# Expert weights of a mixture-of-experts layer: 2 MB loads in 16 KB rows, and a ring split into wide and narrow slots

## The chip, the cores and the metric

The kernel runs on one core of one Trainium2 chip. The metric is the device time of one execution in microseconds (us); lower is better. All data are float32 in the chip's main memory at the start, and the output goes back there. In this document 1 MB of a load is 1,048,576 bytes; the profile's own MB and GB/s are decimal, so that 1 MB at 424 GB/s takes 2.473 us.

## The reference, cut to what matters

Two transformer blocks over 256 tokens of width 1024. The first block and the mixer of the second take the first part of the kernel. What the change touches is the second block's expert layer: 64 experts in 8 groups, each token goes to two experts of one group, and every expert has three matrices of 2 MB each.

```python
def hier_moe(h, rg_w, rg_b, re_w, re_b, w_gate, w_up, w_down):      # 256 tokens, D = 1024
    g_prob = softmax(t @ rg_w + rg_b); p_group, g_sel = top_k(g_prob, 1)
    e_prob = softmax(logits of the chosen group's 8 experts); top_p, top_i = top_k(e_prob, 2)
    gate = p_group * top_p / sum(top_p); expert = g_sel * 8 + top_i
    ...
    def run_block(args):                                           # the tokens of one expert e
        xb = t_pad[tok]
        hb = silu(xb @ w_gate[e]) * (xb @ w_up[e])                 # w_gate, w_up: 64 x [1024, 512]
        return hb @ w_down[e]                                      # w_down: 64 x [512, 1024]
    # the outputs are added per token, weighted by gate; then a residual and a last norm
```

All 64 experts' matrices are read whatever the routing says: 64 x 6 MB = 384 MB.

## The kernel before, in words

The kernel has two kinds of stages. In the first (first block, and the second block's mixer, up to about 725 us) weights of 1 MB come through a **ring** of buffers in on-chip memory, named `raw`: a buffer is taken by `ring_tile`, filled by a load that SyncE (SP) issues, split into a high and a low part (`wh` by ScalarE, `wl` by VectorE), and multiplied three times by TensorE. A buffer is free for the next load when its last split is done. The order of the work on the compute engines is planned by `_Sched`; the order of the loads is simply the order in which the weights are used.

In the second stage, the experts, no weight is split: TensorE multiplies straight from the `raw` buffers. The loads are issued by `load_chunks` (line 1951) in the order of `seq`: for expert e four chunks, gate and up in turn, each [128 partitions x 4 x 512] (one half of a partition's eight rows of the matrix, 8 KB in one piece per partition), and then the two down chunks of expert e - 1, each [128 x 2 x 1024], made of two rows of 4 KB per partition. Every chunk is 1 MB and fits any buffer of the ring. The ring is one list: four buffers `ra`, six `rb` (since the first block's feed-forward), three `rc` (opened when the retention of the mixer, whose last tile is `oc`, is done), one `rd`, the two halves `xh` and `xl` of the transposed input, and, when the mixer's working memory is closed, five `re` and one `rf`: 22 buffers, 22 MB. SP issues loads strictly in order: a load whose buffer is not free holds back all behind it.

Per expert, TensorE does in this order: `gate_up(e)` (64 matmul passes of [128 x 32] by [128 x 256], the first half on the first two chunks, the second half on the other two), for every fourth expert the `gather` of the next four experts' tokens (32 matmuls on `oh`), `down(e - 1)` (32 passes on `gT`), and `turn(e)`, two transposes of the hidden tile `hh` into `gT`. `gate_up(0)` cannot start before the routing is through (the chain of small VectorE steps on tiles `r_...`, then `gather(0)`). For the last expert, `warm(1)` puts a matmul that nobody reads (`wk`) after every second k in `gate_up`, the down matrix comes in three pieces of columns (`LAST`), and `last_down` and the final norm follow.

Of the kernel before, what the change touches and what calls it, by code (L numbers as in the profile page):

```python
# [20 lines left out]
P = 128  # L21
# [5 lines left out]
# ---------------------------------------------------------------- layouts  # L27
# [9 lines left out]
PV["norm2p"] = _o        # feature 8 p + k in column k of partition p  # L37
# [10 lines left out]
def _const_tables():  # L48
    """Tables that depend on shapes alone, one row per partition."""
# [57 lines left out]
# columns of w_in  # L107
# [3 lines left out]
class _Engine:  # L111
    """An engine that also keeps its clock: an estimate of when its queue is through."""
# [34 lines left out]
class _Sched:  # L147
    """Emission order: a background of matrix products, with chains of small steps emitted
    between them as soon as their inputs are estimated to be there."""
# [24 lines left out]
    def lag(self, t):  # L174
        """the chain's result comes t later than its engine's time says."""
        self.end += t

    def step(self, g):
        """one step of g; True if it emitted anything or ended."""
        prev, e0, end0 = self.cur, self.emitted, self.end  # L180
        self.cur, self.end = g, 0.0
        try:
            next(g.g)
            alive = True
        except StopIteration:
# [14 lines left out]
    def force(self):  # L200
        """progress of the chain that is ready first."""
# [34 lines left out]
class _Cat:  # L236
    """k-tiles of several tiles as one."""
# [9 lines left out]
class _X:  # L247
    """a transposed operand as (high, low) parts; `ready` k-tiles of it are written."""
# [15 lines left out]
def kernel(ctx: ExitStack, tc: tile.TileContext, I: dict, out: bass.AP):  # L264
# [21 lines left out]
    # ------------------------------------------------------------ arithmetic helpers  # L286
# [14 lines left out]
    def mm3(o, l, r, start, stop):  # L301
        """o += l.T @ r with l = (high, low), r = (high, low)."""
# [21 lines left out]
    def split(hi, lo, src):  # L324
        """hi = the high part of src; lo = src - hi, a step later."""
# [4 lines left out]
    # ------------------------------------------------------------ constants, small inputs  # L330
# [28 lines left out]
    def warm(n):  # L359
        """products that nobody reads: they keep the tensor engine's clock up while it has to wait."""  # L360
# [4 lines left out]
    # ------------------------------------------------------------ weight stream  # L365
# [4 lines left out]
    def add_ring(pool, n, name, at=0):  # L370
        """n more slots, to be used after the next `at` ones."""
        ring[at:at] = [(pool, "%s%d" % (name, r)) for r in range(n)]

    def ring_tile(shape, name="raw"):
        slot = ring.pop(0)
        ring.append(slot)
        return slot[0].tile(shape, F32, name=name, tag=slot[1], bufs=1)
# [6 lines left out]
    def add_chunk(w, r0, nr, c0, ncol, mode):  # L384
        """rows r0.., columns c0.. of w, as [128, nr/128, ncol]; two pieces, cut by columns or by rows."""
# [38 lines left out]
    def get_piece(held=0):  # L424
        """the next piece, while `held` pieces before it are still to be used."""
# [7 lines left out]
    def convert(m):  # L433
        """the splits of the pieces that follow, piece m being the oldest in use."""
# [87 lines left out]
    # ------------------------------------------------------------ residual -> X^T (high, low), 1/rms  # L522
    def new_x():
        return _X([xpool.tile([P, 8, T], F32R, name="xh", tag="xh"), xpool.tile([P, 8, T], F32R, name="xl", tag="xl")], 0)
# [6 lines left out]
    def xt_steps(src, c, X, gname, ss):  # L531
        """columns c*256.. of src [128, 2, 1024] -> X^T k-tiles 2c, 2c+1, and sums of squares."""
# [24 lines left out]
    def rsqrt_ops(t, dst, src, scale):  # L557
        """dst = (src * scale + eps) ** -0.5: a guess from the bits, then Newton's steps."""
# [12 lines left out]
    def rsqrt_cols(t, dst, src, scale, cols):  # L571
        """the same for a few columns, each a [128, 1] with itself as a scalar: a shorter chain."""
# [55 lines left out]
    def tm_piece(pb, W, X, k0, K, first, last):  # L628
        """pb [128, 2, 256] += X^T.T @ W over k-tiles k0..k0+K."""
# [10 lines left out]
    def need(X, k):  # L640
        """k k-tiles of X; before the next piece is asked for, whose splits would get in their way."""
# [13 lines left out]
    def pair_tm(X, posts):  # L655
        """two chunks, the first halves first: the last k-tiles of X may come late."""
# [23 lines left out]
    # ================================================================ first block: mixer  # L680
# [26 lines left out]
    def norm_sums(srcs, pb):  # L707
        """token-major sums of squares over the 128 partitions: column 8 t + 2 h + i."""
# [17 lines left out]
    def norm_steps(items, inv, name):  # L726
        """items (x [128, 4, 256], gain or None, factor): x scaled in place by its heads' 1/norm."""
# [99 lines left out]
    def smalls():  # L827
        """forget, beta and decay logits, token-major."""
# [47 lines left out]
    # ---------------------------------------------------------------- gated delta rule  # L876
# [6 lines left out]
    def gdn():  # L883
# [5 lines left out]
        # cumulative decay inside chunks of 64  # L889
# [23 lines left out]
        et = smallA.tile([P, 32], F32, name="et")     # exp(gc) | exp(gl - gc) | exp(gl) rows  # L913
# [9 lines left out]
        # rows of beta * decay  # L923
# [4 lines left out]
        # k k^T and (k q^T), chunk by chunk  # L928
# [97 lines left out]
        free("s4", "s4", "g2")        # kbg, vb, U  # L1026
# [48 lines left out]
        free("g2", "g2", "s4", "s4", "s4", "s4")        # aT, S; qg, ktl, wT, u  # L1075

    def gdn_qg():
        """q scaled by exp(gc)."""
# [24 lines left out]
        # token-major k, v  # L1103
# [15 lines left out]
        free("s4", "s4", "s4")        # q, k, v  # L1119
# [6 lines left out]
    def gdn_out(i, po):  # L1126
# [24 lines left out]
        if sc.fin.get("yb", 0) == 1:  # L1151
            free("s4")        # gz
# [77 lines left out]
    def fox(i):  # L1230
# [22 lines left out]
    def fox_all():  # L1253
# [3 lines left out]
        free("s4", "s4", "s4")        # fq, fk, fv  # L1257

    # ---------------------------------------------------------------- stick-breaking, transposed scores
    def stick():  # L1260
# [3 lines left out]
        # banks: key tile 0, heads (0,1) and (2,3), all queries; key tile 1, all heads, queries 128..255  # L1264
# [11 lines left out]
        free("s4", "s4")        # sq, sk  # L1276
# [81 lines left out]
    # ---------------------------------------------------------------- gates x branch outputs, w_out  # L1358
# [32 lines left out]
    def bg_mix():  # L1391
        for n, (y, b, need) in enumerate((("yc", 2, 1), ("ya", 0, 2), ("yb", 1, 2))):
# [19 lines left out]
            free("s4", "s4", "s4", "s4")        # y, gates  # L1412
# [8 lines left out]
    # ================================================================ first block: attention over the memory  # L1421
# [70 lines left out]
    def mq_norm(c):  # L1492
        """1/rms of the queries of heads 2 c, 2 c + 1: column 2 h + i."""
# [55 lines left out]
    def bg_mo():  # L1549
        yield from banks(3, "mm")  # L1550
        pbs, W = [], []
        for c in range(3):        # the first two heads' part first
# [19 lines left out]
    # ================================================================ first block: conv ffn  # L1572
    pools = {}

    def to_ffn():
        a1.close()
        rawB = ctx.enter_context(tc.tile_pool(name="rawB", bufs=1))
        add_ring(rawB, NRB2, "rb", 2)
# [112 lines left out]
    # ================================================================ second block: retention and conv  # L1691
# [141 lines left out]
    def ret_out(n, po):  # L1833
# [17 lines left out]
        if sc.fin["rg"] == 2:  # L1851
            pools["a3r"].close()
            add_ring(ctx.enter_context(tc.tile_pool(name="rawC", bufs=1)), 3, "rc", 8)
# [48 lines left out]
    add_ring(ctx.enter_context(tc.tile_pool(name="rawD", bufs=1)), 1, "rd", 13)  # L1902
    ring[13 + 1:13 + 1] = [(xpool, "xh"), (xpool, "xl")]
# [24 lines left out]
    # expert weights: four chunks for gate and up, two for down, in the order of use  # L1928
    wg, wu, wd = I["w_gate_2"][0], I["w_up_2"][0], I["w_down_2"][0]
    LAST = (0, 512, 768, D)        # the last expert's down matrix comes in pieces of columns  # L1930
    chunks = {}
    nload = [0]
    seq = []
    for e in range(NE + 1):
        seq += [(e, r) for r in range(4) if e < NE] + [(e - 1, r) for r in (4, 5, 6)[:3 if e == NE else 2] if e > 0]

    def load_chunks(upto):
        """loads of expert chunks upto (exclusive); a slot is taken again once its last use is emitted."""
        while nload[0] < min(upto, len(seq)):
            e, r = seq[nload[0]]  # L1940
            if r < 4:
                src = (wg, wu)[r % 2][e].rearrange("(p k) n -> p k n", p=P)[:, (r // 2) * 4:(r // 2) * 4 + 4, :]
# [360 lines left out]
```

## Time and profile before

| what | value |
|---|---|
| median of 3 runs | 1670.82 us (1669.52 to 1933.18) |
| profiled execution, from first to last instruction (its span; no other time of it is given) | 1671.8 us |
| TensorE matmul busy | 1408.8 us, 84% |
| VectorE / ScalarE busy | 648.1 us, 39% / 446.5 us, 27% |
| moved by DMA | 516.74 MB, mean 309 GB/s |

The profile cuts the span into 40 slices of 41.8 us. For each it gives the busy share of an engine in tenths, the clock that TensorE was granted, the busy share of the 16 DMA engines and the GB/s that they moved. Slices 1 to 17 are the first stage, 19 to 40 the experts.

### The profile page before, as it was taken

How to read it: one execution, taken by the hardware profiler on the slowest of the kernel's cores; microseconds unless marked ns; L12 is line 12 of the kernel's file. 1: busy time of each engine (PE TensorE's matmuls, PEld its weight loads, DVE VectorE, ACT ScalarE, POOL GpSimd, SP SyncE). 2: the span in 40 equal slices, each digit the busy share in tenths (PEclk: the TensorE clock that was granted, in tenths of full speed). 3: DMA queues.
4: the chain of work that ended last, by engine and by line, in shares of the span. 5: the costliest groups of instructions: out<-in, count | busy, mean ns of one | idle time of the engine just before them, and what ended most of it. 6: DMA issues, size and time to landing. Idle time of an engine off the chain costs nothing. (4 is left out here: it accounts for less than half of the span.)

```text
span 1671.8 us, 30189 instructions
## 1 busy us (share of the span) xinstructions
PE 1408.8 (84%) x13017; PEld 1066.5 (64%) x13017; DVE 648.1 (39%) x1160; ACT 446.5 (27%) x821; POOL 78.8 (5%) x246
## 2 busy tenths in 40 slices
PE   8999999999999999898867767776786787777685
PEld 7999989989999989875534443443443444344242
DVE  5945356856777767742211111111111111111112
ACT  5643345546555554411100000000000000000001
POOL 1011110131100010200000000000000000000000
PEclk9999999999999999999988887988977987898888
DMA  8543225633855645669999999999999999999995
GB/s 286 175 129 102 77 88 184 208 126 130 301 198 180 216 155 177 237 274 414 423 424 424 424 424 424 424 424 423 423 425 424 424 424 424 424 423 424 424 424 227
DMA packets 170486, 516.74 MB, mean 309 GB/s; under 512 B 9248, under 2 KB 96688, under 8 KB 137584
## 3 DMA queue, kind: packets, MB, share of 16 engines
q1 hardware_dynamic: 169392, 511.90, 77.7%
q0 software_dynamic: 672, 2.66, 0.4%
q8 instruction: 104, 1.70, 0.4%
q10 hardware_dynamic: 288, 0.23, 0.1%
q14 instruction: 30, 0.25, 0.0%
HBM read 513.71 MB, written 1.05 MB: 308 GB/s over the span
## 5 line engine op out<-in xcount | busy, mean ns | idle before, releaser
L288 PE MATMUL pbmm<-raw,xt 128*32 128x256 f32 x4096 | 328.6, 448 | 90.0 <-DMA raw<-in_w_up_dram 73.0
L288 PEld LDWEIGHTS pbmm<-raw,xt 128*32 128x32 f32 x4096 | 156.4, 125 | 247.1 <-DMA raw<-in_w_up_dram 110.9
L122 DVE TENSOR_TENSOR wl<-raw,wh 128x1024 fp32r<-128x1024 f32 x202 | 248.6, 1233 | 129.5 <-PE pbmm L288 81.2
L288 PE MATMUL pbmm<-xh,wh 128*128 128x256 f32 x992 | 285.2, 288 | 0.0
L288 PE MATMUL pbmm<-xl,wh 128*128 128x256 f32 x992 | 279.4, 282 | 0.1
L288 PE MATMUL pbmm<-xh,wl 128*128 128x256 f32 x992 | 278.8, 281 | 0.0
L122 ACT ACTIVATE wh<-raw 128x1024 fp32r<-128x1024 f32 x202 | 213.5, 1060 | 235.1 <-PE pbmm L288 190.2
L122 DVE TENSOR_TENSOR hh<-hh,pbmm 64x256 f32<-64x256 f32 x64 | 27.2, 425 | 464.2 <-ACT hh L122 464.2
L288 PE MATMUL pbmm<-raw,gT 128*32 128x256 f32 (+2 forms) x2112 | 144.7, 401 | 55.7 <-DMA raw<-in_w_down_dram 54.6
L288 PEld LDWEIGHTS pbmm<-xh,wh 128*128 128x128 f32 x992 | 188.9, 190 | 2.1 <-issue 1.2
L288 PEld LDWEIGHTS pbmm<-xl,wh 128*128 128x128 f32 x992 | 188.5, 190 | 1.4 <-issue 0.7
L288 PEld LDWEIGHTS pbmm<-xh,wl 128*128 128x128 f32 x992 | 188.5, 190 | 0.0
L122 ACT ACTIVATE hh<-pbmm 64x256 f32<-64x256 f32 x64 | 24.0, 375 | 513.4 <-PE pbmm L288 513.4
L288 PE MATMUL pbmm<-oh,xres 128*128 128x128 f32 x512 | 131.4, 422 | 30.2 <-DVE oh L122 30.2
L288 PEld LDWEIGHTS pbmm<-oh,xres 128*128 128x128 f32 x512 | 124.5, 334 | 44.9 <-issue 43.5
L288 PEld LDWEIGHTS pbmm<-raw,gT 128*32 128x32 f32 x2112 | 64.9, 116 | 125.4 <-DMA raw<-in_w_down_dram 59.6
L122 DVE COPY ye<-pbmm 32x256 f32<-32x256 f32 (+2 forms) x138 | 56.2, 408 | 193.3 <-ACT ye L122 190.3
L122 ACT COPY ye<-pbmm 32x256 f32<-32x256 f32 x126 | 45.6, 362 | 289.6 <-PE pbmm L288 259.1
L288 PE MATMUL pbfg<-ye,Se 128*128 128x512 f32 (+1 forms) x132 | 65.9, 644 | 10.4 <-DVE ye L122 10.4
L122 DVE TENSOR_TENSOR xt<-pbmm,pv 128x512 f32<-128x512 f32 x32 | 22.1, 692 | 107.0 <-PE pbmm L288 107.0
L288 PEld LDWEIGHTS pbfg<-ye,Se 128*128 128x128 f32 x132 | 24.9, 208 | 39.9 <-DVE ye L122 20.7
L298 PE MATMUL pbmm<-cst,S 128*128 128x128 f32 x32 | 9.7, 400 | 43.2 <-DVE S L122 43.2
(442 smaller groups left out, 1690.6 us busy)
## 6 DMA issues: line engine op xcount, KB each, us to landing
raw<-in_w_up_dram SPq DMA_DIRECT2D x150, 1024.0 KB, 19.6
raw<-in_w_down_dram SPq DMA_DIRECT2D x138, 1024.0 KB, 19.7
raw<-in_w_gate_dram SPq DMA_DIRECT2D x128, 1024.0 KB, 19.7
raw<-in_w_in_dram SPq DMA_DIRECT2D x45, 1024.0 KB, 5.0
raw<-in_w_out_dram SPq DMA_DIRECT2D x4, 1024.0 KB, 5.0
raw<-in_w_mkv_dram SPq DMA_DIRECT2D x4, 1024.0 KB, 5.0
raw<-in_w_o_dram SPq DMA_DIRECT2D x4, 1024.0 KB, 5.2
raw<-in_w_oc_dram SPq DMA_DIRECT2D x2, 1024.0 KB, 5.3
```

The costliest lines, as they stand in the source:

```text
L122: r = f(*a, **k)
L288: PE.matmul(o, l, r, start=start, stop=stop, skip_group_check=True)
L298: PE.transpose(o, i, idt)
```

## The change: what it does

- Gate and up matrices of an expert come as one load each: 2 MB, [128 x 8 x 512], one row of 16 KB per partition. They go into **wide** buffers, which stand in a list of their own, `ring2`: one of `rc`, three of `rb` (the six of before in pairs), one of `xhl` (`xh` and `xl` are now one tile), and, appended later, two of `re`: 7 wide buffers, 14 MB.
- Down matrices still come as two loads of 1 MB, but with the rows of a partition next to each other: one row of 8 KB per partition. `turn` reads the hidden tile with a stride of two to match (not for the last expert, whose down pieces keep their old layout). They go into **narrow** buffers, which stay in `ring`: four `ra`, two `rd`, one `rg`, one `rf`: 8 MB.
- `load_chunks` takes the head of the list that the next load belongs to. If the chunk in that buffer has not been used by the program so far (its key is still in `chunks`), it returns.
- In the first stage the `rb` pairs are used as two halves of one tile.

All instructions of TensorE, VectorE, ScalarE and GpSimd stay in the same order; only SP's loads change.

```diff
+    class _Slot:
+        def __init__(self, pool, tag, wide=None, half=0):
+            self.pool, self.tag, self.wide, self.half, self.key = pool, tag, wide, half, None
+        def tile(self, shape, name):
+            if self.wide is None:
+                return self.pool.tile(shape, F32, name=name, tag=self.tag, bufs=1)
+            if self.half == 0:
+                self.wide["tile"] = self.pool.tile([P, 2, 2048], F32, name=name, tag=self.tag, bufs=1)
+            return self.wide["tile"][:, self.half].rearrange("p (a b) -> p a b", a=shape[1])
...
-        add_ring(rawB, NRB2, "rb", 2)
+        add_ring(rawB, NRB2 // 2, "rb", 2, wide=True)
...
-            add_ring(ctx.enter_context(tc.tile_pool(name="rawC", bufs=1)), 3, "rc", 8)
+            wide["c"] = slots(rawC, 1, "rc", True)
+            add_ring(rawC, 1, "rd", 8)
...
-        seq += [(e, r) for r in range(4) if e < NE] + [(e - 1, r) for r in (4, 5, 6)[:3 if e == NE else 2] if e > 0]
+        seq += [(e, r) for r in range(2) if e < NE] + [(e - 1, r) for r in (4, 5, 6)[:3 if e == NE else 2] if e > 0]
+    ring2 = wide["c"][:1] + [x for x in ring if x.wide is not None and x.half == 0] + [_Slot(xpool, "xhl", {})]
+    ring[:] = [x for x in ring if x.wide is None] + late
-    def load_chunks(upto):
-        while nload[0] < min(upto, len(seq)):
-            e, r = seq[nload[0]]
+    def load_chunks():
+        while seq:
+            e, r = seq[0]
+            rg = ring2 if r < 4 else ring
+            if rg[0].key in chunks:
+                return
+            slot = rg.pop(0)
+            rg.append(slot)
+            slot.key = seq.pop(0)
             if r < 4:
-                src = (wg, wu)[r % 2][e].rearrange("(p k) n -> p k n", p=P)[:, (r // 2) * 4:(r // 2) * 4 + 4, :]
-                t = ring_tile([P, 4, 512])
+                src = (wg, wu)[r][e].rearrange("(p k) n -> p k n", p=P)
+                t = slot.pool.tile([P, 8, 512], F32, name="raw", tag=slot.tag, bufs=1)
...
-                src = wd[e, (r - 4) * 256:(r - 3) * 256, :].rearrange("(k p) n -> p k n", p=P)
-                t = ring_tile([P, 2, D])
+                src = wd[e, (r - 4) * 256:(r - 3) * 256, :].rearrange("(p k) n -> p k n", p=P)
+                t = slot.tile([P, 2, D], "raw")
             SP.dma_start(t, src)
...
-    load_chunks(len(ring))
+    load_chunks()
     warm(31)
     wsp.close()
-    add_ring(rawE, 5, "re")
-    load_chunks(len(ring))
+    ring2 += slots(rawE, 2, "re", True)[::2]
+    load_chunks()
...
-    add_ring(ctx.enter_context(tc.tile_pool(name="rawF", bufs=1)), 1, "rf")
-    NR = len(ring)
-    load_chunks(NR)
+    ring += slots(rawE, 1, "rg") + slots(ctx.enter_context(tc.tile_pool(name="rawF", bufs=1)), 1, "rf")
+    load_chunks()
...
     def gate_up(e):
-        ck_ = [chunks.pop((e, r)) for r in range(4)]
+        w2 = [chunks.pop((e, r)) for r in range(2)]
...
-                w = ck_[(k // 4) * 2 + q // 2]
-                mm(gu[q * 32:(q + 1) * 32, 0:256], xt[:, k, es], w[:, k % 4, (q % 2) * 256:(q % 2) * 256 + 256],
+                mm(gu[q * 32:(q + 1) * 32, 0:256], xt[:, k, es], w2[q // 2][:, k, (q % 2) * 256:(q % 2) * 256 + 256],
                    k == 0, k == 7)
...
-            tr(pt[:, c * 64:(c + 1) * 64], h[64:, c * P:(c + 1) * P], ident[64:, 64:])
+            tr(pt[:, c * 64:(c + 1) * 64], hc[:, c], ident[64:, 64:])
...
     for e in range(NE):
-        load_chunks(4 * e + 2 * max(0, e - 1) + NR)
+        load_chunks()
```

SP's queue before, from the 13th of the expert loads: the end of the 22 loads that fill the ring, and the first two that use a buffer again. The number after `raw` is the buffer's use, and in brackets stand the counters that the load waits for (`DMAHW` the landing of an earlier load, `DVE`, `PE`, `Activation` and `Pool` the engine that used the memory last).

```order
L1951 DMA raw_8187<-in_w_gate_2_dram 128x2048 [waits DMAHW4_49,PE_49]
L1951 DMA raw_8189<-in_w_up_2_dram 128x2048 [waits DMAHW5_49]
L1951 DMA raw_8191<-in_w_down_2_dram 128x2x1024 [waits DMAHW6_49,DVE_49]
L1951 DMA raw_8193<-in_w_down_2_dram 128x2x1024 [waits DMAHW7_49,DVE_49]
L1951 DMA raw_8233<-in_w_gate_2_dram 128x2048 [waits DMAHW0_49,PE_49]
L1951 DMA raw_8235<-in_w_up_2_dram 128x2048 [waits DMAHW1_49]
L1951 DMA raw_8237<-in_w_gate_2_dram 128x2048 [waits DMAHW2_49]
L1951 DMA raw_8239<-in_w_up_2_dram 128x2048 [waits DMAHW3_49]
L1951 DMA raw_8241<-in_w_down_2_dram 128x2x1024 [waits DMAHW4_49]
L1951 DMA raw_8342<-in_w_down_2_dram 128x2x1024 [waits DMAHW5_49,DVE_49,Pool_49]
L1951 DMA raw_8433<-in_w_gate_2_dram 128x2048 [waits DMAHW6_49,PE_49]
L1951 DMA raw_8435<-in_w_up_2_dram 128x2048 [waits DMAHW7_49,PE_49]
```

SP's queue after the change, from its first expert load.

```order
L1985 DMA raw_8144<-in_w_gate_2_dram 128x4096 [waits DMASW2_49,DVE_49,DMAHW0_49,PE_49,Activation_49]
L1985 DMA raw_8146<-in_w_up_2_dram 128x4096 [waits DMAHW1_49,DMAHW2_49,DVE_49,Activation_49]
L1985 DMA raw_8148<-in_w_gate_2_dram 128x4096 [waits DMAHW4_49,DMAHW3_49,DVE_49]
L1985 DMA raw_8150<-in_w_up_2_dram 128x4096 [waits DMAHW6_49,DMAHW5_49,DVE_49]
L1985 DMA raw_8152<-in_w_down_2_dram 128x2048
L1985 DMA raw_8154<-in_w_down_2_dram 128x2048
L1985 DMA raw_8156<-in_w_gate_2_dram 128x4096 [waits PE_49]
L1985 DMA raw_8384<-in_w_up_2_dram 128x4096 [waits DMAHW7_49,DMAHW0_49,PE_49]
L1985 DMA raw_8386<-in_w_down_2_dram 128x2048
L1985 DMA raw_8388<-in_w_down_2_dram 128x2048 [waits DMAHW1_49]
L1985 DMA raw_8390<-in_w_gate_2_dram 128x4096 [waits DMAHW2_49,PE_49]
L1985 DMA raw_8463<-in_w_up_2_dram 128x4096 [waits DMAHW3_49,PE_49]
```

What moved: the eighth load, up of expert 2 (`raw_8384`), takes the buffer of the first one (`raw_8144`, gate of expert 0), and the PE count that it waits for is the last pass of `gate_up(0)` on that buffer; before, the first load that waits for `gate_up(0)` is the 23rd (`raw_8433`, the buffer of `raw_8163`).

SP's queue before, the loads of the last expert with the down matrix of the one ahead of it.

```order
L1951 DMA raw_13354<-in_w_gate_2_dram 128x2048 [waits DMAHW0_49,PE_49]
L1951 DMA raw_13356<-in_w_up_2_dram 128x2048 [waits DMAHW1_49,PE_49]
L1951 DMA raw_13358<-in_w_gate_2_dram 128x2048 [waits DMAHW2_49,PE_49]
L1951 DMA raw_13360<-in_w_up_2_dram 128x2048 [waits DMAHW3_49,PE_49]
L1951 DMA raw_13428<-in_w_down_2_dram 128x2x1024 [waits DMAHW4_49,PE_49]
L1951 DMA raw_13430<-in_w_down_2_dram 128x2x1024 [waits DMAHW5_49,PE_49]
L1951 DMA raw_13432<-in_w_down_2_dram 128x4x512 [waits DMAHW6_49,PE_49]
L1951 DMA raw_13434<-in_w_down_2_dram 128x4x256 [waits DMAHW7_49,PE_49]
L1951 DMA raw_13436<-in_w_down_2_dram 128x4x256 [waits DMAHW0_49,PE_49]
```

The same place after the change.

```order
L1985 DMA raw_13083<-in_w_gate_2_dram 128x4096 [waits DMAHW2_49,PE_49]
L1985 DMA raw_13151<-in_w_up_2_dram 128x4096 [waits DMAHW3_49,PE_49]
L1985 DMA raw_13153<-in_w_down_2_dram 128x2048 [waits DMAHW4_49]
L1985 DMA raw_13155<-in_w_down_2_dram 128x2048 [waits DMAHW5_49]
L1985 DMA raw_13157<-in_w_down_2_dram 128x4x512 [waits DMAHW6_49,PE_49]
L1985 DMA raw_13159<-in_w_down_2_dram 128x4x256 [waits DMAHW7_49,PE_49]
L1985 DMA raw_13232<-in_w_down_2_dram 128x4x256 [waits DMAHW0_49,PE_49]
```

What moved: up's first half no longer comes ahead of gate's second half, so that the first pass on the up matrix has the whole of both in front of it; the 4 MB behind it are the same.

## Rows read from the trace of the kernel before

**Rows 1.** The page's slices: DMA engines' busy tenths, and GB/s.

```profile
DMA  8543225633855645669999999999999999999995
GB/s 286 175 129 102 77 88 184 208 126 130 301 198 180 216 155 177 237 274 414 423 424 424 424 424 424 424 424 423 423 425 424 424 424 424 424 423 424 424 424 227
```

**Rows 2.** Busy time by stretch: stretch, length, engines, then granted clock, DMA share, GB/s.

```profile
730.00:740.00 10.00, 8.70 (x39) 4.58 (x37) 5.75 (x28) 1.81 (x4) 0.00 (x0) 0.89 0.98 411
740.00:750.00 10.00, 9.90 (x91) 8.10 (x90) 3.63 (x16) 0.00 (x0) 0.00 (x0) 1.00 0.37 118
750.00:760.00 10.00, 6.24 (x102) 3.70 (x102) 3.12 (x8) 1.48 (x4) 0.00 (x0) 0.98 0.98 380
1000.00:1200.00 200.00, 147.02 (x1490) 82.46 (x1493) 30.59 (x73) 15.77 (x43) 0.00 (x0) 0.86 1.02 424
```

**Rows 3.** SP's issues in order of time, 640 to 760 us: start, length, what.

```profile
648.89 0.34 SPq L1951 DMA_DIRECT2D raw<-in_w_gate_dram  x1
...
679.43 0.33 SPq L1951 DMA_DIRECT2D raw<-in_w_up_dram  x1
...
705.51 7.22 SPq L1951 DMA_DIRECT2D raw<-in_w_down_dram  x2
...
727.56 10.34 SPq L1951 DMA_DIRECT2D raw<-in_w_down_dram  x2
748.21 0.34 SPq L1951 DMA_DIRECT2D raw<-in_w_gate_dram  x1
749.96 0.38 SPq L1951 DMA_DIRECT2D raw<-in_w_gate_dram  x1
```

**Rows 4.** TensorE in order of time, 736 to 766 us: start, length, what.

```profile
738.43 7.88 PE L288 MATMUL pbmm<-oh,xres 128*128 128x128 f32 x32 [1.30 <-DVE oh L122]
746.24 3.66 PE L288 MATMUL pbmm<-raw,xt 128*32 128x256 f32 x64
...
751.21 3.66 PE L288 MATMUL pbmm<-raw,xt 128*32 128x256 f32 x64
...
760.27 4.98 PE L288 MATMUL pbmm<-raw,xt 128*32 128x256 f32 x64
```

**Rows 5.** DMA, 22 to 30 us, first-stage loads in rows of 1 KB.

```profile
DMA packets 3051, 3.08 MB, mean 385 GB/s; under 512 B 48, under 2 KB 3050, under 8 KB 3051
...
q1 hardware_dynamic: 3051, 3.08, 108.4%
```

**Rows 6.** DMA, 900 to 1600 us, expert loads in rows of 8 KB and 4 KB.

```profile
DMA packets 52671, 296.76 MB, mean 424 GB/s; under 512 B 4518, under 2 KB 4518, under 8 KB 28457
...
q1 hardware_dynamic: 52624, 296.05, 101.2%
```

**Rows 7.** DMA issues of the page: count, KB each, median us to landing.

```profile
raw<-in_w_gate_dram SPq DMA_DIRECT2D x128, 1024.0 KB, 19.7
```

**Rows 8.** TensorE in order of time, 1636 to 1665 us, the last expert.

```profile
1637.32 0.33 PE L298 MATMUL pbfg<-cst,hh 64*128 64x64 f32 x2
...
1641.27 1.92 PE L288 MATMUL pbmm<-raw,xt 128*32 128x256 f32 x12 [1.72 <-DMA raw<-in_w_up_dram]
1643.12 0.61 PE L363 MATMUL pbmm<-wk 128*128 128x512 bf16 x1
1643.66 1.94 PE L288 MATMUL pbmm<-raw,xt 128*32 128x256 f32 x16
...
1646.07 1.56 PE L288 MATMUL pbmm<-raw,xt 128*32 128x256 f32 x16
1647.56 0.39 PE L363 MATMUL pbmm<-wk 128*128 128x512 bf16 x1
1647.88 1.07 PE L288 MATMUL pbmm<-raw,xt 128*32 128x256 f32 x16
...
1653.77 1.08 PE L288 MATMUL pbmm<-raw,gT 128*32 128x128 f32 x32 [0.57 <-DMA raw<-in_w_down_dram]
1655.13 0.65 PE L288 MATMUL pbmm<-raw,gT 128*32 128x64 f32 x32 [0.28 <-DMA raw<-in_w_down_dram]
```

More of the change, by code (lines that the diff above doesn't have):

```diff
@@ L368, with slots, add_ring @@
     ring = []
-    def add_ring(pool, n, name, at=0):
-        ring[at:at] = [(pool, "%s%d" % (name, r)) for r in range(n)]
+    class _Slot:
[7 more added lines that the diff above has]
+            return self.wide["tile"][:, self.half].rearrange("p (a b) -> p a b", a=shape[1])
+    def slots(pool, n, name, wide=False):
+        if not wide:
+            return [_Slot(pool, "%s%d" % (name, r)) for r in range(n)]
+        out = []
+        for r in range(n):
+            w = {}
+            out += [_Slot(pool, "%s%d" % (name, r), w, h) for h in range(2)]
+        return out
+    def add_ring(pool, n, name, at=0, wide=False):
+        ring[at:at] = slots(pool, n, name, wide)
     def ring_tile(shape, name="raw"):
@@ L376, in ring_tile @@
         ring.append(slot)
-        return slot[0].tile(shape, F32, name=name, tag=slot[1], bufs=1)
+        return slot.tile(shape, name)
     rawp = ctx.enter_context(tc.tile_pool(name="rawp", bufs=1))
@@ L523, in new_x @@
     def new_x():
-        return _X([xpool.tile([P, 8, T], F32R, name="xh", tag="xh"), xpool.tile([P, 8, T], F32R, name="xl", tag="xl")], 0)
+        x = xpool.tile([P, 2, 8, T], F32R, name="xhl", tag="xhl")
+        return _X([x[:, 0], x[:, 1]], 0)
     def squares(src, c, ss):
@@ L1689 @@
     spawn(rstd_when(X3, st3, "rstd3"))
+    wide = {}
     rstd3, rstdB3 = st3[1], st3[2]
@@ L1852, in ret_out @@
             pools["a3r"].close()
-            add_ring(ctx.enter_context(tc.tile_pool(name="rawC", bufs=1)), 3, "rc", 8)
+            rawC = ctx.enter_context(tc.tile_pool(name="rawC", bufs=1))
+            wide["c"] = slots(rawC, 1, "rc", True)
+            add_ring(rawC, 1, "rd", 8)
         yield
@@ L1901 @@
     nc.gpsimd.dma_start(wrt, I["wrt"].rearrange("(k p) n -> p k n", p=P))
-    add_ring(ctx.enter_context(tc.tile_pool(name="rawD", bufs=1)), 1, "rd", 13)
-    ring[13 + 1:13 + 1] = [(xpool, "xh"), (xpool, "xl")]
+    late = slots(ctx.enter_context(tc.tile_pool(name="rawD", bufs=1)), 1, "rd")
     plg = []
@@ L1931 @@
     chunks = {}
-    nload = [0]
     seq = []
     for e in range(NE + 1):
-        seq += [(e, r) for r in range(4) if e < NE] + [(e - 1, r) for r in (4, 5, 6)[:3 if e == NE else 2] if e > 0]
-    def load_chunks(upto):
-        while nload[0] < min(upto, len(seq)):
-            e, r = seq[nload[0]]
+        seq += [(e, r) for r in range(2) if e < NE] + [(e - 1, r) for r in (4, 5, 6)[:3 if e == NE else 2] if e > 0]
[10 more added lines that the diff above has]
+            slot.key = seq.pop(0)
             if r < 4:
-                src = (wg, wu)[r % 2][e].rearrange("(p k) n -> p k n", p=P)[:, (r // 2) * 4:(r // 2) * 4 + 4, :]
-                t = ring_tile([P, 4, 512])
+                src = (wg, wu)[r][e].rearrange("(p k) n -> p k n", p=P)
+                t = slot.pool.tile([P, 8, 512], F32, name="raw", tag=slot.tag, bufs=1)
             elif e == NE - 1:
@@ L1946, in load_chunks @@
                 src = wd[e, :, c0:c1].rearrange("(k p) n -> p k n", p=P)
-                t = ring_tile([P, 4, c1 - c0])
+                t = slot.tile([P, 4, c1 - c0], "raw")
             else:
-                src = wd[e, (r - 4) * 256:(r - 3) * 256, :].rearrange("(k p) n -> p k n", p=P)
-                t = ring_tile([P, 2, D])
+                src = wd[e, (r - 4) * 256:(r - 3) * 256, :].rearrange("(p k) n -> p k n", p=P)
+                t = slot.tile([P, 2, D], "raw")
             SP.dma_start(t, src)
-            chunks[e, r] = t
-            nload[0] += 1
-    load_chunks(len(ring))
+            chunks[slot.key] = t
+    load_chunks()
     warm(31)
@@ L2148, in gate_up, with turn @@
         return h
-    def turn(h):
+    def turn(h, e):
         pt = bank("fg", False)
+        hc = h[64:].rearrange("q (c p) -> q c p" if e == NE - 1 else "q (p c) -> q c p", c=2)
         for c in range(2):
-            tr(pt[:, c * 64:(c + 1) * 64], h[64:, c * P:(c + 1) * P], ident[64:, 64:])
+            tr(pt[:, c * 64:(c + 1) * 64], hc[:, c], ident[64:, 64:])
         gT = mb.tile([P, 2, 64], F32, name="gT", tag="gT", bufs=1)
@@ L2231 @@
             warm(3)
-        gT, g0 = turn(h), gT
+        gT, g0 = turn(h, e), gT
         if e % 4 == 1:
```

## The prediction

> **What bounds the kernel now.** I read the slices first. From slice 20 to the end the DMA engines are busy 90% or more and move 423 to 425 GB/s in every slice [rows 1]: the experts are one long load. Next the stretches, to see whether anything else is near its limit there. Of 1000 to 1200 us TensorE is busy 147 at a granted clock of 0.86, against a DMA share of 1.02 [rows 2]. So in this stage the end is set by the bytes still to load when the stream begins, divided by the rate, plus what TensorE does after the last bytes. Every queue edit has to be read as a change to one of these.
>
> When does the stream begin? Not with the first expert load. SP issues that at 648.89 us, and by 737.6 us the 22nd (the row at 727.56 holds two, the second at its end), which fills the last buffer [rows 3]. Then SP stands until 748.21 us [rows 3], while DMA falls to 118 GB/s [rows 2]: it waits for the first half of `gate_up(0)`, which begins at 746.24 us and ends at 749.90 [rows 4]. That in turn waits for the routing and for `gather(0)`, which VectorE releases at 738.43 us [rows 4], not for a load. So at the moment the stream begins, 22 of 384 MB are on board, whatever gaps there were before, and 362 MB are left. At 424 GB/s, 2.473 us for 1 MB, they take 895.2 us; from 750.7 us (748.21 and about 2.5 us until bytes flow, for the stretch from 750 us has 380 GB/s and the one before 118) that leads to 1646. The last pieces land about 9 us later (TensorE waits for the next to last at 1655.13 us [rows 8]); I leave that rest, a slower end of the stream, as it is.
>
> **The change, part by part.**
>
> Fewer buffers are filled ahead. `ring2` holds five wide buffers when loading starts. They take gate and up of experts 0 and 1 and gate of 2; with the two down loads between these, 12 MB. The next load is up of expert 2. Its list stands at `rc`, which holds gate of expert 0; this is still in `chunks`, so `load_chunks` returns. The two wide `re` are appended behind it, so that the two later calls return at once as well. SP is in order, so the narrow buffers stay empty too, and the order of the queue shows the load that comes eighth waiting for TensorE. The memory is as large as before, but 10 MB of it are not used until `gate_up(0)` is done. Nothing hides these 10 MB, for the stream behind is DMA-bound to its end: 10 x 2.473 = **+24.7 us**. That loading starts later (at 679.43 us, when `rc` comes free, where before it was 648.89 [rows 3]) costs nothing: the last release that these 12 MB need is that of the load at 705.51 us [rows 3], and from there 12 MB at full rate would take 30 us, until 736, before `gate_up(0)` at 746.24.
>
> The stream begins a little later. A wide buffer is free when all of its eight k are done, so the first new load goes with the end of `gate_up(0)`, as before's third one at 749.96 us, not at 748.21 [rows 3]: +1.75 at most, less the little that before moved until then. I take **+1.5 us** (1.0 to 1.75). After that SP finds work: u2, both downs of expert 1 and g3 (6 MB, 15 us of DMA) wait for `gate_up(0)` alone; u3, two downs and g4 need `gate_up(1)`, which before ran at 751.21 us [rows 4]; u4 needs `gate_up(2)`, which waits for u2 at some 757 us and takes 4 to 7 us, when DMA has work until about 780. I see no second stop. Later, u(e + 3) needs the end of `gate_up(e)`, with eight loads, 12 MB, queued ahead of it.
>
> Longer rows. What does a row cost beyond its bytes? Two stretches are full of loads, with rows of different length. From 22 to 30 us, 3051 packets carry 3.08 MB [rows 5]: 16 engines x 8 us / 3051 = 41.95 ns for 1009.5 bytes. From 900 to 1600 us, 52671 packets carry 296.76 MB [rows 6]: 16 x 700 / 52671 = 212.6 ns for 5634 bytes. The difference is 0.0369 ns a byte, 27.1 bytes per ns and engine, and what is left is **4.7 ns a packet**. The same with the packets' own durations, which overlap (busy shares of 108.4% and 101.2% of 16 engines [rows 5, 6]), gives 8.3 ns; I take 4.7, since it is elapsed time that the stream saves, and keep 8.3 as the bound. A load's 128 rows lie on 16 engines, 8 on each. A gate or up matrix had 16 packets on an engine and two closing ones, now 8 and one: 9 x 4.7 = 42 ns, for the 123 wide loads behind the start 5.2 us. A down load has 8 instead of 16: 38 ns, for 124 of them 4.7 us. Together **-9.9 us** (-17.4 with 8.3 ns). No row of before has 16 KB packets in SP's queue, so for the wide half the bound on the other side is nothing: -5.3 with the closing packets alone.
>
> The down matrix's new layout costs nothing elsewhere: `turn` has the same two transposes, 0.33 us [rows 8], and TensorE is idle 53 of 200 us there [rows 2]; even if the strided read doubled them, it would be hidden, but for one expert at the end, which keeps the old layout.
>
> The last expert. Until now gate_up(63) did its first half while the second was still coming: its passes began with the up half that came at 1641.27 us, and from 1646.07, when the second half was in, half of the passes were left: 1.56 and 1.07 us with their `wk` matmuls, until 1648.88 [rows 8], 2.8 us. Now all four groups of 16 begin when up is in. TensorE has stood since `turn(62)` at 1637.7 us by then [rows 8], and behind such a wait the groups ran at half clock, 1.94 us and 0.5 to the next, until those from 1646.07 us got faster and those from 1647.88 took 1.07 and 0.3 [rows 8]. All at full clock 5.0 us, all at half 9.8; I take two groups of each, 7.6. That is 4.8 later, of which the two waits for down pieces, 0.57 and 0.28 us [rows 8], take up 0.85, for the 4 MB behind up are the same. **+4.0 us** (1.3 to 6.2).
>
> Sum: 24.7 + 1.5 - 9.9 + 4.0 = +20.3 us, on the span of 1671.8 1692.1. The median of the runs is 1.0 below that span, which I carry over: **1691 us**, 1.2% slower. With all bounds at their low ends, 1.0 - 17.4 + 1.3 + 24.7 = +9.6, 1680; at the high ends, 1.75 - 5.3 + 6.2 + 24.7 = +27.4, 1698.
>
> [...] Each load took 19.7 us from issue to landing [rows 7] with eight under way, 2.46 us of stream for each, which is the time of its bytes alone: a fixed cost per load does not show. [...] For rows without end my fit gives 27.1 x 16 = 434 GB/s, so that no row length wins back the 10 MB. [...]
>
> **The rivals.**
> - *The stream goes to its limit.* If the cost per packet went away whole with rows of 16 KB, 372 MB x 1.0486 / 434 GB/s = 898.8 us instead of 920.0: -21.2, and with 24.7 + 1.5 + 4.0 in all +9.0, 1680 us. For it: a busy share of 101.2% [rows 6] leaves no other loss. Against: halving packets cannot remove all of them.
> - *The wide rows are cut again*, so that the change doesn't do what it says: the page would show 8 KB packets as before, and -5.3 instead of -9.9 gives 1695 us. Nothing in the trace speaks for or against.
> - *The head start is not lost*, because the loads behind the eighth do go out before `gate_up(0)`: -9.9 + 4.0 = -6, 1665 us. The order of the queue speaks against it.
> - *TensorE becomes the bound* (slower by over 2%). Its waits, so far in three or four pieces per expert, gather in one, and each expert begins at half clock, as the last one does [rows 8]. Per expert (14.84 us) it is busy 10.9 at 0.86 [rows 2], 9.4 at full clock. The stream then needs 14.7; TensorE needs more if the mean clock falls below 0.64, and at 0.60 it needs 15.7, 1 us more, for 62 experts 62 us: 1753 us. The 13 us up to the 2% line come at 0.63. For it: half-clock stretches are there already. Against: it slows itself, for work at half clock fills the very wait that lowered it, and 12 MB of queue carry it over single slow experts.
> - *Each load carries a fixed cost* that fewer loads save: for over 2% it would take 53 us against the sum, 0.43 us for each of 123 loads, where 19.7 / 8 leaves nothing beside the bytes [rows 7]. [...]
>
> **How the numbers follow.** The forecast as summed, 1680 to 1698: 0.65. Cut rows, 1695: 0.12. Limit, 1680: 0.06. Head start kept, 1665: 0.05. TensorE, 1715 to 1760: 0.08. Fixed cost per load: 0.01. Else, either side: 0.03. The range of 1677 to 1703 takes in the first three with the tail's spread. Within 2% (1637 to 1704, about what a measurement of this kernel tells from no change) lie the first four and most of the rest: 0.89; slower 0.09, TensorE and a little of the cut rows; faster 0.02.
>
> **What would show it.** SP's issues: seven expert loads from about 679 to 707 us, then none until about 750, and DMA near zero from 725 to 750 us. The stretch 1000 to 1200: 427 to 431 GB/s and fewer than 60% of the packets; TensorE's busy time about as before at a clock of 0.75 or more. `gate_up(0)` at 746 us as now. At the end, 64 passes of gate_up(63) in one piece of 5 to 10 us, and no DMA waits behind it. If the rate is 424, the rows are cut or cost nothing; if it is under 420, or TensorE shows no waits for `raw`, I am wrong about the bound; if SP issues between 710 and 745 us, about the buffers.

## The result, and the profile after

The changed kernel takes **1691.08 us** (median of 4 runs, 1689.73 to 1692.22) against 1671.39 before: ratio **1.0117** [1.0105, 1.0130], 1.2% slower. One of the four runs of before, 1933.18 us, is a slow execution; the ratio uses the fast runs alone, and the other three of before have a median of 1670.82. The profiled run has a span of 1687.3 us and a time of 1689.73, 2.4 us more.

The page's slices of the changed kernel (they answer to [rows 1]): busy tenths of the DMA engines, and GB/s.

```profile
DMA  8533235644755642739999999999999999999994
GB/s 284 175 126 101 76 100 176 206 145 161 257 183 199 221 148 75 277 146 427 429 429 430 428 429 428 428 429 429 428 430 429 428 428 428 430 428 429 429 428 192
```

From slice 20 to the last but one every slice is at 428 to 430 GB/s, where before it was 423 to 425. The stream is faster and the kernel slower, so bytes must be missing ahead of the stream. SP's issues in order of time, 640 to 760 us (for [rows 3]):

```profile
675.96 0.34 SPq L1985 DMA_DIRECT2D raw<-in_w_gate_dram  x1
...
704.99 0.56 SPq L1985 DMA_DIRECT2D raw<-in_w_gate_dram  x1
746.21 0.33 SPq L1985 DMA_DIRECT2D raw<-in_w_up_dram  x1
746.58 0.91 SPq L1985 DMA_DIRECT2D raw<-in_w_down_dram  x2
747.59 0.61 SPq L1985 DMA_DIRECT2D raw<-in_w_gate_dram  x1
751.28 0.33 SPq L1985 DMA_DIRECT2D raw<-in_w_up_dram  x1
```

Seven loads, then nothing for 41 us. TensorE, 735 to 765 us (for [rows 4]), shows what the eighth waited for:

```profile
742.52 3.66 PE L288 MATMUL pbmm<-raw,xt 128*32 128x256 f32 x64
...
747.59 3.66 PE L288 MATMUL pbmm<-raw,xt 128*32 128x256 f32 x64
```

`gate_up(0)` begins at 742.52 and ends at 746.18; at 746.21 SP goes on. Busy time by stretch (columns as in [rows 2]):

```profile
725.00:750.00 25.00, 22.20 (x188) 15.62 (x191) 13.02 (x68) 3.83 (x9) 0.00 (x0) 1.00 0.12 38
...
1000.00:1200.00 200.00, 142.22 (x1423) 82.49 (x1424) 30.52 (x72) 15.40 (x42) 0.00 (x0) 0.82 1.01 428
```

The DMA engines move 38 GB/s for 25 us just ahead of a stage in which they are the bound. In that stage TensorE is busy 142 of 200 us at a granted clock of 0.82: it has room. DMA of 900 to 1600 us (for [rows 6]), and then the page's issues of gate matrices (for [rows 7]):

```profile
DMA packets 27492, 300.05 MB, mean 429 GB/s; under 512 B 3049, under 2 KB 3049, under 8 KB 3049
```

```profile
raw<-in_w_gate_dram SPq DMA_DIRECT2D x64, 2048.0 KB, 29.4
```

There are 52% of the packets of before. The 29.4 us from issue to landing are the time of 12 MB at 429 GB/s, what the prediction had queued ahead of a load. TensorE in order of time, 1645 to 1680 us, the last expert (for [rows 8]):

```profile
1657.60 1.92 PE L288 MATMUL pbmm<-raw,xt 128*32 128x256 f32 x12 [4.11 <-DMA raw<-in_w_up_dram]
...
1659.99 1.94 PE L288 MATMUL pbmm<-raw,xt 128*32 128x256 f32 x16
...
1662.40 1.60 PE L288 MATMUL pbmm<-raw,xt 128*32 128x256 f32 x16
...
1664.25 1.07 PE L288 MATMUL pbmm<-raw,xt 128*32 128x256 f32 x16
...
1669.37 1.53 PE L288 MATMUL pbmm<-raw,gT 128*32 128x128 f32 x64
```

After 4.11 us of waiting for up, all groups of `gate_up(63)` follow in one piece, 1657.60 to 1665.25: two at 1.9 us, then faster. The down passes behind wait for no DMA any more.

### The profile page after: what moved, and what is told of

Its sections match the earlier page's. It is cut to its first block, busy times and chain, and to the rows that moved or that the text cites. A ratio compares the mean times of both kernels' runs of the same rounds, so it can differ in the third digit from the quotient of the medians.

```text
span 1687.3 us, 29786 instructions
## 1 busy us (share of the span) xinstructions
PE 1390.7 (82%) x13017; PEld 1061.3 (63%) x13017; DVE 647.7 (38%) x1160; ACT 446.5 (26%) x821; POOL 77.7 (5%) x246
## 5 line engine op out<-in xcount | busy, mean ns | idle before, releaser
L288 PE MATMUL pbmm<-raw,xt 128*32 128x256 f32 x4096 | 333.6, 459 | 175.9 <-DMA raw<-in_w_up_dram 135.3
L288 PEld LDWEIGHTS pbmm<-raw,xt 128*32 128x32 f32 x4096 | 152.3, 130 | 345.4 <-DMA raw<-in_w_up_dram 163.7
L288 PE MATMUL pbmm<-xhl,wh 128*128 128x256 f32 x1984 | 359.8, 283 | 0.0
L288 PEld LDWEIGHTS pbmm<-xhl,wh 128*128 128x128 f32 x1984 | 305.3, 189 | 3.4 <-issue 2.0
L288 PE MATMUL pbmm<-xhl,wl 128*128 128x256 f32 x992 | 277.8, 280 | 0.3 <-DVE wl L122 0.2
L288 PEld LDWEIGHTS pbmm<-xhl,wl 128*128 128x128 f32 x992 | 187.3, 189 | 0.7 <-DVE wl L122 0.7
L288 PE MATMUL pbmm<-raw,gT 128*32 128x256 f32 (+2 forms) x2112 | 140.6, 381 | 5.4 <-DMA raw<-in_w_down_dram 5.4
L288 PEld LDWEIGHTS pbmm<-raw,gT 128*32 128x32 f32 x2112 | 69.9, 112 | 57.9 <-DMA raw<-in_w_down_dram 12.5
L288 PE MATMUL pbfg<-ye,Se 128*128 128x512 f32 (+1 forms) x132 | 59.7, 593 | 9.3 <-DVE ye L122 9.3
L288 PE MATMUL pbmm<-wh,xhl 128*128 128x256 f32 x256 | 49.4, 286 | 0.9 <-DVE xhl L122 0.9
L288 PEld LDWEIGHTS pbfg<-ye,Se 128*128 128x128 f32 x132 | 22.4, 189 | 35.4 <-DVE ye L122 19.2
## 6 DMA issues: line engine op xcount, KB each, us to landing
raw<-in_w_down_dram SPq DMA_DIRECT2D x138, 1024.0 KB, 29.4
raw<-in_w_gate_dram SPq DMA_DIRECT2D x64, 2048.0 KB, 29.4
raw<-in_w_up_dram SPq DMA_DIRECT2D x64, 2048.0 KB, 29.4
```

The costliest lines, as they stand in the source:

```text
L288: PE.matmul(o, l, r, start=start, stop=stop, skip_group_check=True)
```

## The experiments

The theory: 10 MB that are not on board at `gate_up(0)` cost their time at the stream's rate, a split last expert costs 4 us, and fewer packets give back about 10. Against it stood a loss or gain per load whatever its size, and a stream at another rate.

Two spans cannot be subtracted safely: `gate_up(0)` began anywhere from 741.34 to 746.24 us in the eleven profiles of the table, and that of before is the latest (the changed kernel alone has 742.52 and 744.46). What the change does to the stream shows behind this point, so the table counts from it to the end of the span. The same kernel profiled twice gives 944.8 and 944.7.

| kernel | median us | ratio to before [95%] | `gate_up(0)` begins | span | from there to the end |
|---|---|---|---|---|---|
| before | | | 746.24 | 1671.8 | 925.6 |
| after | 1691.08 | 1.0117 [1.0105, 1.0130] | 742.52 | 1687.3 | 944.8 |
| after_again | 1691.50 | 1.0120 [1.0103, 1.0136] | 744.46 | 1689.2 | 944.7 |
| re_first | 1676.12 | 1.0039 [1.0024, 1.0055] | 741.34 | 1671.1 | 929.8 |
| fill_22 | 1667.33 | 0.9980 [0.9971, 0.9989] | 745.84 | 1667.2 | 921.4 |
| before_head12 | 1697.25 | 1.0167 [1.0152, 1.0183] | 744.55 | 1693.7 | 949.2 |
| wide_8k | 1693.78 | 1.0141 [1.0125, 1.0156] | 744.19 | 1691.3 | 947.1 |
| before_down8k | 1667.64 | 0.9976 [0.9968, 0.9985] | 744.44 | 1665.1 | 920.7 |
| tail_halves | 1688.62 | 1.0103 [1.0088, 1.0118] | 743.48 | 1683.9 | 940.4 |
| fill_22_tail | 1664.60 | 0.9954 [0.9941, 0.9967] | 745.81 | 1662.3 | 916.5 |
| wide_parity | 1691.82 | 1.0120 [1.0103, 1.0137] | 745.54 | 1690.8 | 945.3 |

**re_first**, the two `re` buffers at the front of `ring2`, so that 18 MB can be on board:

```diff
-    ring2 += slots(rawE, 2, "re", True)[::2]
+    ring2[0:0] = slots(rawE, 2, "re", True)[::2]
```

> The changed kernel, but the two wide re buffers are put ahead of the list when they are opened, so that up of expert 2, the downs of expert 1 and gate of expert 3 go out before gate_up(0): 18 MB on board instead of 12. Theory (what is on board when the stream begins decides): 6 MB x 2.447 us = 14.7 us less than the changed kernel, about 1676 us; SP issues 11 expert loads before gate_up(0) and stops then. Rival (TensorE's work in one burst per expert, or the rows of 16 KB, cost the time): within 2 us of the changed kernel, 1691.

SP's issues of re_first around its stop, 700 to 760 us:

```profile
722.30 0.33 SPq L1985 DMA_DIRECT2D raw<-in_w_up_dram  x1
722.67 0.91 SPq L1985 DMA_DIRECT2D raw<-in_w_down_dram  x2
723.62 0.91 SPq L1985 DMA_DIRECT2D raw<-in_w_gate_dram  x1
745.02 0.33 SPq L1985 DMA_DIRECT2D raw<-in_w_up_dram  x1
```

These four loads, 6 MB, follow the seven of after, and then SP stands until `gate_up(0)` ends. Measured 1676.12 us, and 15.0 us less than after from `gate_up(0)` on. Six MB, moved only by the place of two buffers in a list.

**fill_22**, the same for the narrow buffers, and four down loads moved ahead so that all 22 buffers fill:

```diff
+    ahead = [(2, 4), (2, 5), (3, 4), (3, 5)]
+    seq = [x for x in seq if x not in ahead]
+    seq[seq.index((3, 1)):seq.index((3, 1))] = ahead
...
-    ring2 += slots(rawE, 2, "re", True)[::2]
+    ring2[0:0] = slots(rawE, 2, "re", True)[::2]
...
-    ring += slots(rawE, 1, "rg") + slots(ctx.enter_context(tc.tile_pool(name="rawF", bufs=1)), 1, "rf")
+    ring[0:0] = slots(rawE, 1, "rg") + slots(ctx.enter_context(tc.tile_pool(name="rawF", bufs=1)), 1, "rf")
```

> As the run with the re buffers first, and the downs of experts 2 and 3 are loaded ahead of up of expert 3, into narrow buffers that stood empty (the rg and rf buffers also go to the head of their list): 22 MB on board, as in the kernel before. Theory: 10 MB x 2.447 = 24.5 us less than the changed kernel, 1666 to 1667 us, which is about 4.5 us below the kernel before (rows -9.9, start +1.5, last expert +4). Rival (burst or rows cost the time): 1691, or at least not below the kernel before.

SP's issues of fill_22, 700 to 760 us:

```profile
726.82 0.33 SPq L1988 DMA_DIRECT2D raw<-in_w_up_dram  x1
...
728.88 8.56 SPq L1988 DMA_DIRECT2D raw<-in_w_down_dram  x4
749.53 0.33 SPq L1988 DMA_DIRECT2D raw<-in_w_up_dram  x1
```

SP now stands from 737 to 749 us, as before did. Of 725 to 750 us the DMA engines use a share of 0.90:

```profile
725.00:750.00 25.00, 21.84 (x159) 15.82 (x157) 13.08 (x67) 4.55 (x11) 0.53 (x2) 0.93 0.90 367
```

Measured 1667.33 us, 23.4 less than after from `gate_up(0)` on, for 10 MB. With its head start back, the change is a small gain.

**before_head12**, the other side: the kernel before, all its rows as they were, with 12 loads ahead of `gate_up(0)` instead of 22.

```diff
-    load_chunks(len(ring))
+    load_chunks(12)
...
-    load_chunks(len(ring))
...
-    load_chunks(NR)
...
-        load_chunks(4 * e + 2 * max(0, e - 1) + NR)
+        if e == 1:
+            ring.insert(0, ring.pop(10))
+        if e > 0:
+            load_chunks(4 * e + 2 * max(0, e - 1) + NR)
```

> The kernel before, with its 1 MB loads and its rows, but only 12 loads ahead of gate_up(0): the 13th takes the buffer of the first and so waits for gate_up(0), the others follow it. Theory: 10 MB x 2.473 = 24.7 us more than the kernel before, 1696 us. Rival (burst or rows): nothing of the change's rows or loads is in it, so 1671 us.

SP's issues of before_head12 around the gap, 690 to 760 us:

```profile
702.91 0.34 SPq L1951 DMA_DIRECT2D raw<-in_w_up_dram  x1
746.51 0.33 SPq L1951 DMA_DIRECT2D raw<-in_w_gate_dram  x1
```

Measured 1697.25 us, 1.67% slower than before: the gap alone makes the whole loss, 23.6 us from `gate_up(0)` on, with no wide buffer in the program.

**before_down8k**, the kernel before with down rows of 8 KB and the strided `turn`, one part alone:

```diff
-                src = wd[e, (r - 4) * 256:(r - 3) * 256, :].rearrange("(k p) n -> p k n", p=P)
+                src = wd[e, (r - 4) * 256:(r - 3) * 256, :].rearrange("(p k) n -> p k n", p=P)
...
-    def turn(h):
+    def turn(h, e):
+        hc = h[64:].rearrange("q (c p) -> q c p" if e == NE - 1 else "q (p c) -> q c p", c=2)
...
-            tr(pt[:, c * 64:(c + 1) * 64], h[64:, c * P:(c + 1) * P], ident[64:, 64:])
+            tr(pt[:, c * 64:(c + 1) * 64], hc[:, c], ident[64:, 64:])
```

> The kernel before with one part of the change alone: down loads with rows of 8 KB in place of two of 4 KB (and the strided read in turn that goes with it). Nothing in the buffers or the order of the loads moves. Theory (4.7 ns a packet): 124 x 8 x 4.7 ns = 4.7 us less than the kernel before, about 1667 us; with the 8.3 ns of the packets' own durations 8.2 us less, 1663. Rival (row length does nothing while loads are queued): 1671 us.

DMA of before_down8k, 900 to 1600 us:

```profile
DMA packets 40908, 298.29 MB, mean 426 GB/s; under 512 B 4539, under 2 KB 4539, under 8 KB 4539
```

Measured 1667.64 us; -4.0 us by the ratio, -4.9 from `gate_up(0)` on. Against [rows 6] there are 11763 packets fewer and 1.53 MB more in the same 700 us. At the prediction's 0.0369 ns a byte, 1.53 MB are 56.5 us of one engine; over 11763 packets, 4.8 ns each.

**wide_8k**, the changed kernel with each wide load in two of 8 KB rows (the first half of every partition's row, then the second):

```diff
-            SP.dma_start(t, src)
+            if r < 2:
+                for h in (slice(0, 4), slice(4, 8)):
+                    SP.dma_start(t[:, h], src[:, h])
+            else:
+                SP.dma_start(t, src)
```

> The changed kernel, each gate and up matrix loaded into the same wide buffer by two loads of 1 MB with rows of 8 KB instead of one with 16 KB. Theory (4.7 ns a packet): 123 x 9 x 4.7 ns = 5.2 us more than the changed kernel, 1696 us, and 426 GB/s instead of 429 in the stream; with 8.3 ns 9.2 us more. Rival (rows of 16 KB cost time, or whole matrices make TensorE late): faster than the changed kernel or the same, 1685 to 1691 us.

DMA of wide_8k, 900 to 1600 us:

```profile
DMA packets 40916, 298.32 MB, mean 426 GB/s; under 512 B 4542, under 2 KB 4542, under 8 KB 4542
```

Measured 1693.78 us, 2.2 under the expectation. The rate is the expected one: 13424 packets more than after and 1.73 MB less, again 4.8 ns a packet, so 5.3 us on 123 loads. Only 2.3 of these show from `gate_up(0)` to the end. The rest is at the last expert, which here begins with the first half of up, 1 MB or 2.5 us of stream earlier:

```profile
1662.02 1.92 PE L288 MATMUL pbmm<-raw,xt 128*32 128x256 f32 x12 [3.76 <-DMA raw<-in_w_up_dram]
```

From `gate_up(0)` to this line are 917.8 us, in after to 1657.60 are 915.1: 2.7 more, which is 5.3 less 2.5. From there to the end of the span are 29.3 us, in after 29.7. No run of its own tests this.

**wide_parity**, two loads again, but with rows of 16 KB: the even partitions, then the odd ones. Twice the loads, data rows as in after.

```diff
-            SP.dma_start(t, src)
+            if r < 2:
+                for h in range(2):
+                    SP.dma_start(t[h:P:2], src[h:P:2])
+            else:
+                SP.dma_start(t, src)
```

> As the run in which each gate and up matrix came in two loads of 64 partitions (which was far slower, 2534 us), but the two loads take the even and the odd partitions in place of the lower and the upper half; rows of 16 KB, 1 MB a load, as many loads as in the kernel before. [...] If any load of 64 rows is slow, the time is again near 2500 us, and the question of a cost per load stays with the other runs.

DMA of wide_parity, 900 to 1600 us:

```profile
DMA packets 28955, 299.85 MB, mean 428 GB/s; under 512 B 4565, under 2 KB 4565, under 8 KB 4565
```

Measured 1691.82 us, beside 1691.50 of **after_again**, the changed kernel run once more on that chip (its expectation below). 128 more loads cost 0.6 us by the profiles (945.3 against 944.7), what the closing packets alone should cost (128 x 4.8 ns): no fixed cost per load shows in a queue that is never empty (428 GB/s from 900 to 1600 us).

> The changed kernel as it is, on the chip of the run beside it, as its anchor: 1.2% above the kernel before, 1691 us.

**wide_64p**, meant as the same test with the loads cut between partitions 63 and 64:

```diff
-            SP.dma_start(t, src)
+            if r < 2:
+                for h in (slice(0, 64), slice(64, 128)):
+                    SP.dma_start(t[h], src[h])
+            else:
+                SP.dma_start(t, src)
```

> The changed kernel, each gate and up matrix loaded by two loads of 1 MB, each 64 partitions with rows of 16 KB: the size and the number of the loads of the kernel before, the rows of the change. Theory (the cost is per packet, not per load): one more closing packet for each of 123 matrices, +0.6 us, 1692 us, the same within the measurement. [...]

Busy time by stretch of wide_64p:

```profile
1000.00:1200.00 200.00, 87.77 (x750) 49.35 (x752) 15.65 (x37) 7.70 (x21) 0.00 (x0) 0.69 0.99 229
```

Measured **2533.81 us** (2426.45 to 2551.68): a complete miss. A share of 0.99 moves 229 GB/s. It said nothing on the cost per load, which is why wide_parity followed; what it did say stands in the last section.

**tail_halves**, the changed kernel, but the last expert's gate and up come as four halves in the old order:

```diff
-            SP.dma_start(t, src)
+            if r < 2 and e == NE - 1:
+                SP.dma_start(t[:, 0:4], src[:, 0:4])
+                if r == 1:
+                    SP.dma_start(chunks[e, 0][:, 4:8], wg[e].rearrange("(p k) n -> p k n", p=P)[:, 4:8])
+                    SP.dma_start(t[:, 4:8], src[:, 4:8])
+            else:
+                SP.dma_start(t, src)
```

> The changed kernel, but the gate and up matrices of the last expert alone come as four loads of 1 MB in the order of the kernel before (first halves, then second halves), so that gate_up(63) can do its first half while the second is still coming. Theory (last expert +4.0 us, 2.9 by the difference of the two traces): 3 to 4 us less than the changed kernel, about 1687.5 us, with half of the 64 passes done before the second half of up is in. Rival (the last expert's work is hidden behind the down loads): 1691 us.

TensorE of tail_halves in order of time, 1645 to 1685 us:

```profile
1653.44 1.06 PE L288 MATMUL pbmm<-raw,xt 128*32 128x256 f32 x12 [1.61 <-DMA raw<-in_w_up_dram]
...
1658.34 1.06 PE L288 MATMUL pbmm<-raw,xt 128*32 128x256 f32 x12 [1.64 <-DMA raw<-in_w_up_dram]
...
1659.65 1.07 PE L288 MATMUL pbmm<-raw,xt 128*32 128x256 f32 x16
...
1665.89 1.08 PE L288 MATMUL pbmm<-raw,gT 128*32 128x128 f32 x32 [0.67 <-SPq L2143]
1667.24 0.65 PE L288 MATMUL pbmm<-raw,gT 128*32 128x64 f32 x32 [0.27 <-SPq L2143]
```

Once the last half of up is there, 2.3 us of passes are left (1658.34 to 1660.65) instead of 7.65, and the short waits before the down pieces are back (0.67 and 0.27 us). 7.65 - 2.3 - 0.94 = 4.4 us, which is what the count from `gate_up(0)` shows (940.4 against 944.8); the ratios differ by 1.4 thousandths, 2.3 us, and their intervals overlap. With two waits of 1.6 us in the place of one of 4.11, TensorE also kept a granted clock of 1.00, where after has 0.50. The passes on the first halves of gate and up by stretch, in the kernel after and then in tail_halves (the granted clock is the third number from the end):

```profile
1658.00:1662.00 4.00, 4.00 (x30) 1.17 (x22) 0.00 (x0) 0.00 (x0) 0.00 (x0) 0.50 0.70 273
```

```profile
1653.00:1656.00 3.00, 2.56 (x30) 1.00 (x30) 0.00 (x0) 0.00 (x0) 0.00 (x0) 1.00 1.03 409
```

**fill_22_tail**, fill_22 with the edit of tail_halves:

> The run with 22 MB on board and the four loads for the last expert together. Theory: the parts add up, 24.5 + 3.5 us less than the changed kernel, about 1663 us, 8 us (0.5%) below the kernel before. Rival (parts do not add): no better than the run with 22 MB alone, 1666 to 1667 us.

Measured 1664.60 us, ratio 0.9954 [0.9941, 0.9967]: faster than both kernels, by 0.5% and 1.6%, and 4.9 us less than fill_22 from `gate_up(0)` on. By the ratios it is 4.3 us less than fill_22, and here the two intervals do not overlap.

## Why the prediction was right, point by point

| term | predicted us | measured us | by |
|---|---|---|---|
| head start of 10 MB lost | +24.7 | +23.6 | before_head12 against before |
| stream begins later | +1.5 | +0.7 to 1.3 | bytes moved in the 20 us from the start of `gate_up(0)` |
| fewer packets | -9.9 | -10.1 | 4.8 ns by three pairs of kernels, on 2099 packets of an engine |
| last expert | +4.0 | +4.4 to 4.9 | tail_halves; fill_22_tail |
| sum, from `gate_up(0)` to the end | +20.3 | +19.2 | the two profiles |

With about the middle of the two ranges, the four measured terms make 23.6 + 1.0 - 10.1 + 4.6 = +19.1, close to the difference in the profiles.

For the second term, the next load goes 3.69 us after the start of `gate_up(0)`, where before it went 1.97 after it, 1.7 us earlier. By the bytes moved, less than that is lost. The first 20 us from the start of `gate_up(0)`, in before and after, then in before_down8k and wide_8k (the last number is GB/s):

```profile
746.24:766.24 20.00, 16.15 (x255) 8.84 (x258) 6.49 (x24) 2.22 (x6) 0.00 (x0) 0.91 0.85 328
742.52:762.52 20.00, 16.26 (x255) 9.01 (x258) 6.48 (x24) 2.22 (x6) 0.00 (x0) 0.91 0.78 313
744.44:764.44 20.00, 16.25 (x273) 9.42 (x276) 6.76 (x25) 2.59 (x7) 0.00 (x0) 1.00 0.86 337
744.19:764.19 20.00, 15.91 (x265) 9.14 (x264) 6.74 (x25) 2.59 (x7) 0.00 (x0) 1.00 0.78 310
```

The first pair is 0.30 MB apart, 0.7 us of stream; the second, whose streams later run at the same 426 GB/s, 0.54 MB or 1.3 us. The term was a little smaller than predicted.

The head start's size is the least sharp: by the ratio the same pair gives 27.9 us (25.4 to 30.6), and fill_22 against after 23.4 by the profiles, 22.9 by the ratios. The price of 24.7 lies between them. The pair with fill_22 mixes in the second term, for there the DMA engines were still at the last of the 22 MB when `gate_up(0)` began (the share of 0.90 above, and 1.01 from 746 to 750 us), so that its stream never stopped. That before_head12 gives 4 us more by its runs than by its profile is explained only in part: its profiled run, 1696.03 us, is the fastest of its four and 1.2 under their median, and in all ten pairs of the table with before the ratio gives more than the profiles, by 0.4 to 2.4 us in the other nine, so that the one profile of before seems to be about 1 us long behind `gate_up(0)` too. The rest stays open.

The packet term came from stretches that differ in more than row length, and the choice of 4.7 over 8.3 ns decided it; before_down8k and wide_8k confirm it for both kinds of row, with 4.8 (before against after is the third pair). `gate_up(63)` takes 7.65 us (7.6 predicted).

**One step was off, and the forecast did not show it.** That 1691 came out within 0.1 us is luck. I took `gate_up(0)` to stay at 746 us and the median to lie 1.0 below the span. Both come from a single profile of before, the latest of eleven in its first stage; here the profiled run's own time lies 2.4 above its span. The span was predicted as 1692.1 and is 1687.3; the median is 3.8 above it, not 1.0 below. The two slips cancel, and what carries the result is the difference: +20.3 predicted, +19.7 between the medians, 17.5 to 21.7 by the interval of the ratio. That interval is far narrower than the 2% that the prediction took a measurement to tell from no change.

The rivals. *Head start kept*: refuted by the seven loads. *Rows cut again*: refuted by 27492 packets against 40916 in wide_8k. *Stream to its limit*, 434 GB/s by the prediction's fit: it is 429. *TensorE as the bound*: its mean clock fell only from 0.86 to 0.82, busy 142 us of 200; the prediction put the loss of 2% at 0.63. *Fixed cost per load*: refuted by wide_parity, where 128 more loads cost 0.6 us in all. The prediction's reading of [rows 7] could not have refuted it: with eight loads always under way, 19.7 us are eight loads at the stream's own rate, 2.47 us each, and a cost per load would be part of that rate.

## What to carry to other kernels

Where a stage is bound by its loads to the end, price a change of buffers by one question first: how many bytes are on board when the first consumer starts? Two lists of buffers behind one in-order queue have one head that can block both (here for 41 us); put the buffers that are free at that moment in front, and let the order of the loads follow. And when a change is worth 1%, count from an event that the change does not move, not from the start of the profile.

## What the runs showed of the hardware that was not expected

That the packet price would be the same from 4 KB to 16 KB rows had only been assumed; it is, 4.8 ns in all three pairs of kernels at the prediction's 0.0369 ns a byte, so that the rate goes 424, 426, 429 GB/s as rows become longer.

Loads of 64 neighbouring partitions run at less than half of the rate (an estimate of 194 GB/s beside 428), although the next load in the queue goes to the other 64. DMA of wide_64p, 900 to 1600 us:

```profile
DMA packets 16046, 165.87 MB, mean 237 GB/s; under 512 B 2529, under 2 KB 2529, under 8 KB 2529
```

An expert's 6.29 MB take 26.5 us at 237 GB/s; its two down loads of 128 partitions, 2.10 MB, take 4.9 at the 428 of the other kernels; so the 4.19 MB of gate and up take 21.6: 194 GB/s. Taking every second partition instead, also 64 in each load, runs at 428. It is thus neither the number of partitions nor of loads, but which partitions a load has; what makes the difference no run shows.
